# FFN up product of a decoder step as seven half-size block products, with activations and residual through DRAM

## The chip, the cores and the metric

The kernel runs on one core of a Trainium2 chip. The metric is the device time of one execution in microseconds. The core's engines, as the profile names them: PE (TensorE, matmuls; PEld its weight loads), DVE (VectorE), ACT (ScalarE), POOL (GpSimd) and SP (SyncE, which only issues transfers). Each runs its own instructions in order and waits for others through semaphores.

## What is computed

One layer of a decoder for a prompt of 1024 tokens and 8 samples of 8 tokens, 1088 columns in all, with D = 1024 and a hidden width of 4096. The change touches the second half of the layer:

```python
def _layer_tail(x, attn, pool, gate1, shift2, scale2, gate2, norm2_g, w_out, w_up, w_down):
    mix = jnp.concatenate([attn, pool], axis=-1).astype(x.dtype) @ w_out
    x = x + gate1 * mix
    h = rms_norm(x, norm2_g) * (1 + scale2) + shift2
    f = jnp.square(jax.nn.relu(h @ w_up)) @ w_down
    return x + gate2 * f
```

Gates, shifts and scales come from a conditioning vector: one for the prompt, one for each sample.

## The kernel before

Everything is stored with features on the 128 partitions and tokens along the columns. A product in full precision is made of three matmuls on 32-bit operands: each operand is split in a rounded high part and the remainder, and high x high, low x high and high x low are summed in PSUM. `gemm` (L238 to L247) walks over the k tiles of 128 rows and issues the three passes for each column chunk; `CHUNKS` cuts the 1088 columns into 512, 288 and 288, since one PSUM bank holds 512. `load_w` and `split_w` (L143 to L153) fetch a weight tile of 512 KB on SP's queue, copy its high part on ScalarE (L146) and subtract on VectorE (L147); four raw buffers and three pairs of split ones (`NRAW`, `NWF`) rotate.

The tail of the layer begins with the out projection, `out_tile`: eight tiles m on the first 512 columns ("a"), then eight on the other 576 ("b"). `add_gated` (L828 to L836) adds the gated result to the residual `X`, which stays in SBUF to the end, and the squares are summed into `acc2` for the norm. `rstd_of` (L198 to L215) makes 1/rms with one matmul by ones per chunk, Ln and Exp on ScalarE and a Newton step on VectorE. `h2_prompt` (L855 to L859) makes the FFN's input, high and low part, for one k. For the first 512 columns this is done while the "b" tiles run. For the others the norm comes after the last "b" tile, and three up tiles on the first 512 columns (`up_a`) stand in front of it.

Then `up(ff)` makes one of 32 tiles of 128 hidden features: `gemm` over eight k tiles, relu on ScalarE from PSUM (L926), square on VectorE (L927), split (L930, L931) into `fh`, `fl`, which stay in SBUF. Four such tiles make a group; `down(gq)` multiplies the group with its part of `w_down` for each of the eight output tiles m and adds the gated result to `X`. Up tiles and down groups alternate, eight groups in all. `windows(b)` copies two caches of a sample from DRAM to DRAM on POOL's queue, 4080 KB each, one pair per group; a copy of one column to `mark` makes it wait for the group's first tile.

The order of instructions outside the blocks named `manual_schedule` is made by a planner that hoists what is ready; inside such a block the engines named keep the program's order.

## Time and profile before

| | us |
|---|---|
| median of 3 runs | 1374.87 |
| lowest and highest of them | 1372.66, 1382.95 |
| the profiled execution, its own time | 1385.76 |
| span of that execution, first to last instruction | 1384.0 |
| mean granted TensorE clock in it | 0.978 |

The profile is of one execution. Its page gives the busy time of each engine, the chain of waits that ended last, and groups of instructions by line, each with its count, busy time, mean and idle time in front. The timeline lists instructions by start; an entry "x3" is three of a kind merged, and its second figure is the time from the first one's start to the last one's end. A duration holds the engine's latency, so that the next instruction of an engine can begin before it is over: what one costs on a busy engine is the distance between starts.

### The profile page before, as it was taken

What the parts mean: (1) busy time and instruction counts of PE and PEld (TensorE: products, weight loads), DVE (VectorE), ACT (ScalarE), POOL (GpSimd) and SP (SyncE); (2) the same over time, 40 slices, a digit from 0 to 9 for tenths busy, and PEclk for the clock granted to TensorE, in tenths of its full rate; (3) what the DMA queues carried; (4) which work ended last, traced back from release to release, by engine and by line L of the source; (5) the groups of instructions that cost most, each with busy time, mean ns of one, the idle gap of its engine ahead of it and who ended that gap; (6) DMA issues with size and microseconds to landing.
All of it is one profiled execution on the core that took longest, in us unless ns stands there. A gap on an engine that the chain in (4) does not pass through costs nothing.

```text
span 1384.0 us, 21247 instructions
## 1 busy us (share of the span) xinstructions
PE 1325.9 (96%) x9060; PEld 1112.8 (80%) x9060; DVE 584.5 (42%) x1120; ACT 390.1 (28%) x660; POOL 119.0 (9%) x175
## 2 busy tenths in 40 slices
PE   3698999998999999999999999999999999999998
PEld 1485777894665567999999999999999999999998
DVE  5643233314656565577332433432433324334333
ACT  6232030224766653435202202112012012021120
POOL 3201002611212000000000000000000000000000
PEclk9899799998999999999999999999999999999999
DMA  9686433427767563482961541721814615411002
GB/s 322 209 112 170 133 124 125 157 93 287 249 208 268 174 232 113 133 282 70 338 207 46 186 149 47 260 74 45 274 46 133 201 46 186 149 47 46 31 33 97
DMA packets 48719, 211.09 MB, mean 153 GB/s; under 512 B 6432, under 2 KB 6688, under 8 KB 47600
## 3 DMA queue, kind: packets, MB, share of 16 engines
q1 hardware_dynamic: 44752, 137.17, 30.3%
q0 software_dynamic: 3872, 72.56, 16.6%
q8 instruction: 71, 1.16, 0.3%
q14 instruction: 24, 0.20, 0.0%
...
## 4 chain that ended last, share of the span: by engine, by line
PE 90%; DMA 4%; DVE 3%; ACT 2%; issue 1%; SPq 0%; DVEq 0%; ACTq 0%
PE dn L245 9%; PE dn L243 9%; PE dn L247 9%; PE up L245 9%; PE up L247 9%; PE up L243 9%; PE z L243 5%; PE z L247 5%; PE z L245 4%; PE po L715 2%; PE pt L705 2%; PE S L660 2%; PE spo L618 1%; PE pa L101 1%; PE sl L572 1%; PE ob L247 1%
## 5 line engine op out<-in xcount | busy, mean ns | idle before, releaser
L831 DVE SCALAR_TENSOR_TENSOR X<-dn,aT,X 128x512 f32<-128x512 f32 (+2 forms) x192 | 98.4, 568 | 204.5 <-PE dn L247 204.5
L863 POOL COPY mark<-fh 128x1 f32<-128x1 f32 x7 | 8.5, 1218 | 561.9 <-ACT fh L930 561.9
L931 DVE TENSOR_TENSOR fl<-r,fh 128x1088 fp32r<-128x1088 f32 x32 | 41.3, 1292 | 35.5 <-ACT fh L930 35.5
L528 ACT ACTIVATE L<-L,m 128x128 f32<-128x128 f32 (+7 forms) x64 | 49.1, 770 | 19.2 <-DVE m L532 19.2
L708 ACT COPY PT<-pt 128x512 f32<-128x512 f32 (+1 forms) x80 | 41.7, 541 | 39.2 <-PE pt L705 30.4
L705 PE MATMUL pt<-cpk,L 128*128 128x128 f32 x288 | 45.4, 284 | 2.6 <-ACT PT L708 1.5
L930 ACT CAST fh<-r 128x1088 fp32r<-128x1088 f32 x32 | 35.4, 1105 | 44.1 <-DVE r L927 44.1
L705 PEld LDWEIGHTS pt<-cpk,L 128*128 128x128 f32 x288 | 31.2, 141 | 18.0 <-issue 10.9
L245 PE MATMUL dn<-fh,wd_3l 128*128 128x288 f32 (+1 forms) x192 | 43.4, 328 | 0.0
L243 PE MATMUL dn<-fh,wd_3h 128*128 128x288 f32 (+1 forms) x192 | 43.4, 328 | 0.0
L247 PE MATMUL dn<-fl,wd_3h 128*128 128x288 f32 (+1 forms) x192 | 43.4, 328 | 0.0
L243 PE MATMUL dn<-fh,wd_1h 128*128 128x288 f32 (+1 forms) x192 | 42.5, 328 | 0.0
L245 PE MATMUL dn<-fh,wd_1l 128*128 128x288 f32 (+1 forms) x192 | 42.5, 328 | 0.0
L247 PE MATMUL dn<-fl,wd_1h 128*128 128x288 f32 (+1 forms) x192 | 42.3, 328 | 0.0
L245 PE MATMUL dn<-fh,wd_0l 128*128 128x288 f32 (+1 forms) x192 | 42.3, 328 | 0.0
L243 PE MATMUL dn<-fh,wd_0h 128*128 128x288 f32 (+1 forms) x192 | 42.2, 328 | 0.0
L245 PE MATMUL dn<-fh,wd_2l 128*128 128x288 f32 (+1 forms) x192 | 42.2, 328 | 0.0
L243 PE MATMUL dn<-fh,wd_2h 128*128 128x288 f32 (+1 forms) x192 | 42.2, 328 | 0.0
L247 PE MATMUL dn<-fl,wd_2h 128*128 128x288 f32 (+1 forms) x192 | 42.2, 328 | 0.0
L247 PE MATMUL dn<-fl,wd_0h 128*128 128x288 f32 (+1 forms) x192 | 42.1, 328 | 0.0
L927 DVE TENSOR_TENSOR r<-r 128x1088 f32<-128x1088 f32 x32 | 41.1, 1286 | 0.0
L532 DVE CUSTOM_DVE_ANT_0 L<-S,fs 128x384 f32<-128x384 f32 (+5 forms) x64 | 32.0, 538 | 18.7 <-PE S L660 18.5
...
## 6 DMA issues: line engine op xcount, KB each, us to landing
out_kw<-in_cache_k POOLq DMA_DIRECT2D x8, 4080.0 KB, 15.8
out_vw<-in_cache_v POOLq DMA_DIRECT2D x8, 4080.0 KB, 29.2
wa<-in_w_ada SPq DMA_DIRECT2D x48, 512.0 KB, 4.7
kc<-in_kc SPq DMA_DIRECT2D x40, 512.0 KB, 5.1
vc<-in_vc SPq DMA_DIRECT2D x40, 512.0 KB, 4.9
...
fs<-gscr SPq DMA_DIRECT2D x8, 512.0 KB, 7.7
```

Source lines behind the costliest of these rows:

```text
L243: mm(pt[:, :n], wh[:, kw], xh(k, c0, n), start=st, stop=False)
L245: mm(pt[:, :n], wl[:, kw], xh(k, c0, n), start=False, stop=False)
L247: mm(pt[:, :n], wh[:, kw], xl(k, c0, n), start=False, stop=sp)
L528: last["act"] = S.activation(L[:, :n], L[:, :n], AF.Exp, bias=negm, scale=-1.0, accum_out=sm)
L532: V.tensor_tensor_reduce(out=L[:, c0:c0 + n], in0=pt, in1=bias, scale=-1.0, scalar=(3.0e38 if prev is None else prev), op0=ALU.add, op1=AL ...
L660: mm(pts[a][:, :nm], w[r, qc], m[r, c0:c0 + nm], start=(x == 0), stop=(x == 2))
L705: nc.tensor.transpose(pt[:, n * P:(n + 1) * P], u["L"][:, a, ii * nk0 + j * P:ii * nk0 + (j + 1) * P], ident)
L708: later(0, lambda: S.copy(PT[:, :n * P], pt[:, :n * P]))
L831: V.scalar_tensor_tensor(X[:, m, c0:c0 + npr], pt[:, :npr], aT[:, base + m, 0:1], X[:, m, c0:c0 + npr], ALU.mult, ALU.add)
L927: V.tensor_tensor(r, r, r, ALU.mult)
L930: S.copy(fh, r)
L931: V.tensor_sub(fl, r, f(fh))
```

## The change

The up product H = W h is cut in 2 x 2 blocks: W by hidden features (ff and ff + 16) and by k (the first and last four k tiles), h by k and by columns (two halves of 544, `T2`, each in two chunks of 272, `NC`). For each of 16 pairs of hidden tiles the four blocks of the result are made of seven block products (Strassen's scheme in Winograd's form) in place of eight. `prod(m, n)` is one of them, 4 k tiles x 3 passes x 2 chunks = 24 matmuls. Products 1, 6, 7 and 4 of a pair add up in two PSUM banks (X), 5 and 3 in two others (Y), 2 in two more (Z); `hold` copies a sum at a certain point from PSUM to SBUF, `result` adds it to another, squares the relu and writes the tile to DRAM (`uscr`) on POOL's queue. `up_w` makes the weight sums (g = 0: none, 1 and 2: two additions of 512 columns, 3: none, half a tile) and their splits.

The sums of h (T1 to T4) are made once: T1 from both column halves of the first four k tiles, T2 and T4 from those and the last four, T3 from all. They stay in SBUF for all 16 pairs in the space of `X`, so the residual is written to DRAM (`xscr`) by `out_tile` and read back as `X3`. The first two pairs are interleaved product by product, in an order written by hand for PE, DVE and ACT, with the norm of the second half and the making of T1 to T4 between the products (`lagged` issues its steps k by k, each later step `lag` turns behind). From m = 2 on the planner orders the pairs. `down` runs after all of up; its activations are loaded four at a time from `uscr` and split then. The out projection now runs on halves of 544 columns as two chunks of 272. Four cache windows go with pairs 3, 6, 9 and 12, three with down groups 0, 2 and 4.

```diff
+T2 = T // 2
+NC = T2 // 2
+K2 = KD // 2
...
+    XQ = {(a, b): xp.tile([P, K2, T2], F32, tag=f"q{a}{b}", name=f"X{a}{b}") for b in range(2) for a in range(2)}
+    def X(k, c0, n):
+        h = c0 // T2
+        return XQ[k // K2, h][:, k % K2, c0 - h * T2:c0 - h * T2 + n]
+    for b in range(2):
+        for k in range(KD):
+            nc.sync.dma_start(X(k, b * T2, T2), i["xT"][k][:, b * T2:(b + 1) * T2])
+    rstd2 = xp.tile([P, T], F32, tag="rstd2", name="rstd2")
...
+    xscr = tc.dram_tile([KD, P, T], F32, name="xscr")
+    uscr = tc.dram_tile([NFF, P, T], F32, name="uscr")
+    bp = tc.alloc_tile_pool(name="bp", bufs=1, side="right", reuse_waits="tile")
+    B1 = [[bp.tile([P, K2, T2], F32R, tag=f"B{k}{n}", name=f"B{k}{n}") for n in "hl"] for k in range(2)]
...
+        G.dma_start(xscr[m][:, a0:a1], X(m, a0, a1 - a0))
+    def split(hi, lo, src):
+        S.copy(hi, src)
+        V.tensor_sub(lo, src, f(hi))
+    def h2_rows(k, half):
+        c0 = half * T2
+        n = min(T2, SEQ - c0)
+        x = X(k, c0, n)
+        V.scalar_tensor_tensor(x, x, A2[:, k, 0:1], rstd2[:, c0:c0 + n], ALU.mult, ALU.mult)
+        S.activation(x, x, AF.Identity, bias=aT[:, 24 + k, 0:1])
...
+    HALF = [((c, NC), (c + NC, NC)) for c in (0, T2)]
     for m in range(KD):
-        out_tile(m, CHUNKS[:1], "a")
-    out_tile(0, CHUNKS[1:], "b")
-    rstd_of(acc2, rstd2, CHUNKS[:1], "n2a")
+        out_tile(m, HALF[0], "a")
+    out_tile(0, HALF[1], "b")
+    rstd_of(acc2, rstd2, HALF[0], "n2a")
     for m in range(1, KD):
-        out_tile(m, CHUNKS[1:], "b")
+        out_tile(m, HALF[1], "b")
         if m == 1:
             windows(0, rstd2[:, 0:1])
             for k in range(KD):
...
-    rstd_of(acc2, rstd2, CHUNKS[1:], "n2b")
...
+                h2_rows(k, 0)
+                split(B1[k // K2][0][:, k % K2], B1[k // K2][1][:, k % K2], X(k, 0, T2))
...
+    raws, wts = {}, {}
+    def up_raw(m):
+        raws[m] = []
+        for x in range(2):
+            raw = wpool.tile([P, 1024], F32, tag="raw", name=f"wu{m}_{x}r", bufs=NRAW)
+            nc.sync.dma_start(raw, i["w_up"][m + x * NFF // 2])
+            raws[m].append(raw)
+    def up_w(m, g):
+        top, bot = raws[m]
+        a11, a12, a21, a22 = top[:, :512], top[:, 512:], bot[:, :512], bot[:, 512:]
+        if g == 0:
+            src, n = top, 1024
+        elif g == 3:
+            src, n = a22, 512
+        elif g == 1:
+            src, n = wpool.tile([P, T], F32, tag="tmp", name=f"ws{m}", bufs=2)[:, :1024], 1024
+            V.tensor_add(src[:, :512], a21, a22)
+            V.tensor_sub(src[:, 512:], src[:, :512], a11)
+            s2[m] = src[:, 512:]
+        else:
+            src, n = top, 1024
+            V.tensor_sub(a11, a11, a21)
+            V.tensor_sub(a12, a12, s2[m])
+        hi = wpool.tile([P, 1024], F32R, tag="wf", name=f"wu{m}_{g}h", bufs=NWF)
+        lo = wpool.tile([P, 1024], F32R, tag="wf", name=f"wu{m}_{g}l", bufs=NWF)
+        S.copy(hi[:, :n], src)
+        V.tensor_sub(lo[:, :n], src, f(hi[:, :n]))
+        wts[m, g] = hi, lo
+    s2, ops = {}, {1: (0, 0), 2: (0, 512), 5: (1, 0), 6: (1, 512), 7: (2, 0), 3: (2, 512), 4: (3, 0)}
+    bs2 = {1: B1[0], 2: B1[1]}
+    banks, held = {}, {}
+    def bank(m, x):
+        if (m, x) not in banks:
+            banks[m, x] = [ps(f"u{x}{m}_{c}", "px" if x == "X" else "pyz") for c in range(2)]
+        return banks[m, x]
+    def hold(m, n, src):
+        held[m, n] = []
+        for c in range(2):
+            t = fr.tile([P, NC], F32, tag=f"held{n}{c}", name=f"h{n}_{m}_{c}", bufs=1 if n == 1 else 2)
+            S.copy(t, src[c][:, :NC])
+            held[m, n].append(t)
+    def result(m, x, half, src, with_):
+        r = fr.tile([P, T2], F32, tag="rt", name=f"r{m}_{x}{half}", bufs=NRT)
+        for c in range(2):
+            dst = r[:, c * NC:(c + 1) * NC]
+            if with_ is None:
+                S.copy(dst, src[c][:, :NC])
+            else:
+                V.tensor_add(dst, src[c][:, :NC], held[m, with_][c])
+        V.scalar_tensor_tensor(r, r, 0.0, r, ALU.max, ALU.mult)
+        G.dma_start(uscr[m + x * NFF // 2][:, half * T2:(half + 1) * T2], r)
+    START = {1: "X", 5: "Y", 2: "Z"}
+    HOME = {1: "X", 6: "X", 7: "X", 4: "X", 5: "Y", 3: "Y", 2: "Z"}
+    def prod(m, n):
+        x = HOME[n]
+        g, w0 = ops[n]
+        hi, lo = wts[m, g]
+        bh, bl = bs2[n]
+        outs = bank(m, x)
+        for k in range(K2):
+            kw = slice(w0 + k * P, w0 + (k + 1) * P)
+            for w, b in ((hi, bh), (lo, bh), (hi, bl)):
+                for c in range(2):
+                    mm(outs[c][:, :NC], w[:, kw], b[:, k, c * NC:(c + 1) * NC], start=(START.get(n) == x and k == 0 and w is hi and b is bh),
+                       stop=(k == K2 - 1 and b is bl), skip_group_check=(n in (6, 7, 3, 4)))
+        if n == 1:
+            hold(m, 1, outs)
+        elif n == 5:
+            hold(m, 5, outs)
+        elif n == 6:
+            hold(m, 6, outs)
+        elif n == 2:
+            result(m, 0, 0, outs, 1)
+        elif n == 7:
+            result(m, 1, 1, outs, 5)
+        elif n == 3:
+            result(m, 0, 1, outs, 6)
+        else:
+            result(m, 1, 0, outs, None)
...
+    for m in range(2):
+        up_raw(m)
+        up_w(m, 0)
+    up_w(0, 1)
...
+    bs2.update({5: (T1h, T1l), 6: (T2h, T2l), 7: (T3h, T3l)})
...
+    with tc.manual_schedule(engines={mybir.EngineType.PE, mybir.EngineType.DVE, mybir.EngineType.Activation}):
+        prod(0, 1)
+        vt = wpool.tile([P, T], F32, tag="tmp", name="n2bv", bufs=2)
+        vv, tv = vt[:, :T2], vt[:, T2:]
+        for c0, n in HALF[1]:
+            pp = ps(f"n2b_{c0}", "pyz")
+            mm(pp[:, :n], ones, acc2[:, c0:c0 + n], start=True, stop=True)
+            V.tensor_scalar(vv[:, c0 - T2:c0 - T2 + n], pp[:, :n], 1.0 / D, EPS, ALU.mult, ALU.add)
+        S.activation(tv, vv, AF.Ln)
+        S.activation(rstd2[:, T2:], tv, AF.Exp, scale=-0.5)
+        newton(rstd2[:, T2:], vv, tv)
+        prod(0, 2)
+        rsb = rstd2[:, SEQ:T].rearrange("p (b t) -> p b t", t=TS).unsqueeze(1).to_broadcast([P, K2, NB, TS])
+        def samples(a):
+            V.tensor_tensor(xsq[a], xsq[a], rsb, ALU.mult)
+            V.tensor_tensor(xsq[a], xsq[a], bs_seq(A2, K2 * a), ALU.mult)
+            V.tensor_tensor(xsq[a], xsq[a], bs_seq(aT, 24 + K2 * a), ALU.add)
+        samples(0)
+        lagged((0, lambda j: h2_rows(j, 1)),
+               (1, lambda j: V.tensor_sub(B(j, 0), B(j, 1), B(j, 0))),
+               (1, hi_of(T1h, lambda j: B(j, 0))),
+               (2, lo_of(T1h, T1l, lambda j: B(j, 0))))
+        prod(1, 1)
+        up_w(0, 2)
+        prod(1, 2)
+        up_w(1, 1)
+        prod(0, 5)
+        samples(1)
+        lagged((0, lambda j: h2_rows(K2 + j, 1)),
+               (1, lambda j: V.tensor_sub(B(j, 0), B(K2 + j, 1), B(j, 0))),
+               (1, hi_of(T2h, lambda j: B(j, 0))),
+               (2, lambda j: V.tensor_sub(B(K2 + j, 0), B(K2 + j, 0), B(j, 0))),
+               (2, lo_of(T2h, T2l, lambda j: B(j, 0))))
+        prod(1, 5)
+        prod(0, 6)
+        lagged((0, lambda j: V.tensor_sub(B(j, 1), B(K2 + j, 1), B(j, 1))),
+               (0, hi_of(T3h, lambda j: B(j, 1))),
+               (1, lo_of(T3h, T3l, lambda j: B(j, 1))))
+        prod(1, 6)
+        prod(0, 7)
+        up_w(1, 2)
+        B4h, B4l = [xp.tile([P, K2, T2], F32R, tag=t, name=n) for t, n in (("q00", "B4h"), ("q01", "B4l"))]
+        bs2[3] = B4h, B4l
+        lagged((0, hi_of(B4h, lambda j: B(K2 + j, 1))), (0, lo_of(B4h, B4l, lambda j: B(K2 + j, 1))))
+        prod(1, 7)
+        prod(0, 3)
+        up_w(0, 3)
+        T4h = xp.tile([P, K2, T2], F32R, tag="q11", name="T4h")
+        bs2[4] = T4h, T4l
+        lagged((0, hi_of(T4h, lambda j: B(K2 + j, 0))), (0, lo_of(T4h, T4l, lambda j: B(K2 + j, 0))))
+        prod(1, 3)
+        prod(0, 4)
+        up_w(1, 3)
+    up_raw(2)
+    up_w(2, 0)
+    prod(1, 4)
+    up_w(2, 1)
...
+    NM = NFF // 2
+    for m in range(2, NM):
+        last = m == NM - 1
+        if not last:
+            up_raw(m + 1)
+        for n in (1, 5, 6, 2, 7, 3, 4) if not last else (1, 2, 5, 6, 7, 3, 4):
+            prod(m, n)
+            if n == 1 and m in (3, 6, 9, 12):
+                windows(m // 3, held[m, 1][0][:, 0:1])
+            if n == 5:
+                up_w(m, 2)
+            elif n == 2 and not last or last and n == 6:
+                up_w(m, 3)
+            elif n == 7 and not last:
+                up_w(m + 1, 0)
+            elif n == 3 and not last:
+                up_w(m + 1, 1)
...
+    def load_f(ff, pool):
+        raw = fb.tile([P, T], F32, tag="fraw", name=f"f{ff}r", bufs=FG)
+        nc.sync.dma_start(raw, uscr[ff])
+        fh = pool.tile([P, T], F32R, tag="fh", name=f"fh{ff}", bufs=FG)
+        fl = pool.tile([P, T], F32R, tag="fl", name=f"fl{ff}", bufs=FG)
+        split(fh, fl, raw)
+        fs_[ff] = (fh, fl)
...
+    for ff in range(FG):
+        load_f(ff, fa)
+    X3 = fb.tile([P, KD, T], F32, tag="X3", name="X3")
     for k in range(KD):
...
-        fh = fr.tile([P, T], F32R, tag="fh", name=f"fh{ff}", bufs=NFR)
-        fl = fr.tile([P, T], F32R, tag="fl", name=f"fl{ff}", bufs=NFR)
...
+        nc.sync.dma_start(X3[:, k, :], xscr[k])
...
+            if mp == 0 and gq + 1 < NFF // FG:
+                for ff in range((gq + 1) * FG, (gq + 2) * FG):
+                    load_f(ff, fa if gq % 2 else fb)
...
     for gq in range(NFF // FG):
-        while nxt < min(NFF, (gq + 1) * FG + 1):
-            up(nxt)
-            nxt += 1
...
-            windows(gq + 1, f(fs_[gq * FG][0][:, 0:1]))
         down(gq)
-    fr.release()
+        if gq in (0, 2, 4):
+            windows(5 + gq // 2, f(fs_[(gq + 2) * FG - 1][0][:, 0:1]))
...
-NFR = 5
+NRT = 4
```

## Rows read from the trace of the kernel before

**Rows 1.** The page: busy time of each engine, and the chain that ended last, by engine.

```profile
PE 1325.9 (96%) x9060; PEld 1112.8 (80%) x9060; DVE 584.5 (42%) x1120; ACT 390.1 (28%) x660; POOL 119.0 (9%) x175
...
PE 90%; DMA 4%; DVE 3%; ACT 2%; issue 1%; SPq 0%; DVEq 0%; ACTq 0%
```

**Rows 2.** The windows view: a stretch in us, its length, then busy us and count of PE, PEld, DVE, ACT, POOL, the granted clock, the DMA engines' busy share and GB/s. The first stretch is a part of the "b" tiles, the second the whole FFN.

```profile
590.00:600.00 10.00, 10.00 (x77) 10.00 (x76) 10.00 (x18) 4.68 (x7) 0.00 (x0) 1.00 0.98 325
...
618.30:1384.00 765.70, 761.84 (x4614) 692.97 (x4612) 290.52 (x477) 146.56 (x204) 15.03 (x21) 1.00 0.38 123
```

**Rows 3.** The timeline: start us, length us, engine, line, what. First the "a" tiles' ends by VectorE's addition, then TensorE in a "b" tile, the next one, the first up tile, and two down tiles that lie two apart.

```profile
533.83 0.75 DVE L831 SCALAR_TENSOR_TENSOR X<-oa,aT,X 128x512 f32<-128x512 f32 x1 [3.36 <-PE oa L247]
...
539.27 0.75 DVE L831 SCALAR_TENSOR_TENSOR X<-oa,aT,X 128x512 f32<-128x512 f32 x1 [2.75 <-PE oa L247]
...
605.49 0.43 PE L243 MATMUL ob<-mixh,wob6h 128*128 128x288 f32 x2
...
611.89 0.43 PE L243 MATMUL ob<-mixh,wob7h 128*128 128x288 f32 x2
...
618.29 0.39 PE L243 MATMUL up<-h2ah,wu0h 128*128 128x512 f32 x1
...
785.84 0.67 PE L243 MATMUL dn<-fh,wd_1h 128*128 128x512 f32 x3
...
797.76 0.67 PE L243 MATMUL dn<-fh,wd_2h 128*128 128x512 f32 x3
```

**Rows 4.** The timeline around the second half's norm, on VectorE (the last out tile's reads of PSUM, and the Newton steps), TensorE and ScalarE.

```profile
618.51 0.87 DVE L831 SCALAR_TENSOR_TENSOR X<-ob,aT,X 128x288 f32<-128x288 f32 x2
619.30 0.22 DVE L834 TENSOR_TENSOR gs<-ob,aT 128x64 f32<-128x64 f32 x1
...
623.89 1.13 PE L205 MATMUL n2b<-acc,cpk 128*128 128x288 f32 x4
624.64 0.61 PE L243 MATMUL up<-h2ah,wu1h 128*128 128x512 f32 x1
...
625.59 1.28 ACT L209 ACT_TABLE_LOAD   x1 [4.03 <-DVE n2bv L206]
...
627.59 1.28 ACT L212 ACT_TABLE_LOAD   x1
...
631.19 0.76 DVE L135 SCALAR_TENSOR_TENSOR rstd<-n2bt,rstd 128x576 f32<-128x576 f32 x1
```

**Rows 5.** Groups by line and form, VectorE then ScalarE: busy us, mean ns of one | idle before.

```profile
L931 DVE TENSOR_TENSOR fl<-r,fh 128x1088 fp32r<-128x1088 f32 x5 | 6.4, 1291 | 3.5 <-ACT fh L930 3.5
...
L926 ACT ACTIVATE r<-up 128x288 f32<-128x288 f32 x10 | 3.5, 408 | 0.0
...
L146 ACT CAST wu0h<-wu0r 128x1024 fp32r<-128x1024 f32 x1 | 1.0, 1049 | 4.9 <-DMA wu0r<-in_w_up 4.9
...
L908 ACT CAST h2bh<-hs 128x512 fp32r<-128x512 f32 x1 | 0.6, 623 | 0.5 <-DVE hs L906 0.5
```

**Rows 6.** The timeline of VectorE: starts of a subtraction of 512 columns and its next, of a PSUM read of 288 and its next, of a weight subtraction of 1024 and its next, and of a 512-column tensor-tensor and its next.

```profile
592.89 0.74 DVE L859 SCALAR_TENSOR_TENSOR h2al<-h2p,aT,h2ah 128x512 fp32r<-128x512 f32 x1
593.55 0.51 DVE L831 SCALAR_TENSOR_TENSOR X<-ob,aT,X 128x288 f32<-128x288 f32 x1
593.98 0.74 DVE L857 SCALAR_TENSOR_TENSOR h2p<-X,A,rstd 128x512 f32<-128x512 f32 x1
...
601.37 1.23 DVE L147 TENSOR_TENSOR wob7l<-wob7r,wob7h 128x1024 fp32r<-128x1024 f32 x1
602.51 0.22 DVE L836 TENSOR_TENSOR X<-X,gs 128x64 f32<-128x64 f32 x1
...
631.98 0.69 DVE L903 TENSOR_TENSOR hs<-X,rstd 128x512 f32<-128x512 f32 x1
632.59 0.74 DVE L857 SCALAR_TENSOR_TENSOR h2p<-X,A,rstd 128x512 f32<-128x512 f32 x1
```

**Rows 7.** The windows view (columns as in rows 2) of a stretch early in the kernel, where TensorE has nothing to do for 3.8 us.

```profile
129.00:132.80 3.80, 0.00 (x0) 0.00 (x0) 3.73 (x4) 0.00 (x0) 0.00 (x0) 0.90 1.00 378
132.80:136.00 3.20, 3.11 (x18) 0.83 (x18) 2.51 (x7) 2.13 (x4) 0.00 (x0) 0.50 0.07 27
...
148.00:152.00 4.00, 4.00 (x14) 3.58 (x14) 0.00 (x0) 0.00 (x0) 0.53 (x1) 0.50 0.93 332
152.00:156.00 4.00, 4.00 (x24) 3.63 (x23) 1.23 (x1) 1.05 (x1) 0.00 (x0) 0.93 0.32 129
```

**Rows 8.** DMA issues: out<-in, issuing queue, count, KB each, median us from issue to landing.

```profile
out_kw<-in_cache_k POOLq DMA_DIRECT2D x8, 4080.0 KB, 15.8
out_vw<-in_cache_v POOLq DMA_DIRECT2D x8, 4080.0 KB, 29.2
...
wd_1r<-in_w_down SPq DMA_DIRECT2D x8, 512.0 KB, 3.7
...
wu1r<-in_w_up SPq DMA_DIRECT2D x1, 512.0 KB, 22.7
```

**Rows 9.** The timeline of SP's queue at the out projection's start: a weight load (which comes after X in the program) and X's eight.

```profile
503.37 0.33 SPq L152 DMA_DIRECT2D woa4r<-in_w_out  x1
...
509.37 4.09 SPq L820 DMA_DIRECT2D X<-in_xT  x8
```

More of the change, by code (lines that the diff above doesn't have):

```diff
@@ L835, in add_gated, with out_tile @@
                             aT[:, base + m, 1:9].unsqueeze(2).to_broadcast([P, NB, TS]), ALU.mult)
-            V.tensor_add(X[:, m, SEQ:T], X[:, m, SEQ:T], t.rearrange("p b t -> p (b t)"))
+            x = X(m, SEQ, NS)
+            V.tensor_add(x, x, t.rearrange("p b t -> p (b t)"))
     acc2 = nat("acc2")
-    rstd2 = xp.tile([P, T], F32, tag="rstd2", name="rstd2")
-    def out_tile(m, chunks, name, split=None):
+    def out_tile(m, chunks, name):
         a0, a1 = chunks[0][0], chunks[-1][0] + chunks[-1][1]
@@ L893, in body @@
-    rstd_of(acc2, rstd2, CHUNKS[1:], "n2b")
-    up_a(1)
-    up_a(2)
+                h2_rows(k, 0)
+                split(B1[k // K2][0][:, k % K2], B1[k // K2][1][:, k % K2], X(k, 0, T2))
+    pools[""].release()
+    pools[""] = tc.alloc_tile_pool(name="psum4", bufs=1, space=PSUM, reuse_waits="tile")
+    raws, wts = {}, {}
[5 more added lines that the diff above has]
+            raws[m].append(raw)
@@ new lines, in body, with lagged @@
+    bs2.update({5: (T1h, T1l), 6: (T2h, T2l), 7: (T3h, T3l)})
+    xsq = [XQ[a, 1][:, :, SEQ - T2:].rearrange("p k (b t) -> p k b t", t=TS) for a in range(2)]
+    hi_of = lambda hi, src: lambda j: S.copy(hi[:, j], src(j))
+    lo_of = lambda hi, lo, src: lambda j: V.tensor_sub(lo[:, j], src(j), f(hi[:, j]))
+    B = lambda k, half: X(k, half * T2, T2)
+    def lagged(*stages):
+        for t in range(K2 + max(lag for lag, _ in stages)):
+            for lag, st in stages:
+                if 0 <= t - lag < K2:
+                    st(t - lag)
@@ new lines, in body @@
+    bp.release()
+    fa = tc.alloc_tile_pool(name="fa", bufs=1, side="right", reuse_waits="tile")
+    fs_ = {}
+    def load_f(ff, pool):
[5 more added lines that the diff above has]
+        fs_[ff] = (fh, fl)
+    fr.release()
+    pools[""].release()
@@ L934, in down @@
+    pools[""] = tc.alloc_tile_pool(name="psum5", bufs=8, space=PSUM, reuse_waits="tile")
+    fb = tc.alloc_tile_pool(name="fb", bufs=1, side="left", reuse_waits="tile")
+    for ff in range(FG):
+        load_f(ff, fa)
+    X3 = fb.tile([P, KD, T], F32, tag="X3", name="X3")
+    for k in range(KD):
+        nc.sync.dma_start(X3[:, k, :], xscr[k])
     def down(gq):
```

79 lines of the change are left out of this document (15 added, 64 removed).

## Prediction

> **What bounds the kernel now.** I read the page's busy lines and the windows first: over the span TensorE is busy 1325.9 of 1384.0 us [rows 1], and from the first up product (618.3) to the end 761.84 of 765.70, at a granted clock of 1.00; VectorE is busy only 290.5 us there and ScalarE 146.6 [rows 2]. The chain of waits agrees: 90% of what ended last is TensorE [rows 1]. So the FFN stage is bound by the number and spacing of its matmuls, and there is no idle time to win back; a change gains only by fewer or narrower matmuls, and loses by every gap that it opens.
>
> Next the timeline, for the spacing. A 512-column matmul of the out projection costs 5.44/24 = 226.7 ns (tile to tile, 533.83 to 539.27), a 288-column one 6.40/48 = 133.3 ns (605.49 to 611.89), and the mixed group 512+288+288 of the down product 11.92/24 = 496.7 ns (785.84 to 797.76) [rows 3]. The straight line through the first two is N/2.4 + 13.3 ns. Up and down are 64 tiles of 24 groups: 64 x 11.92 = 762.9 us. 618.3 + 762.9 leaves 2.8 us of 1384.0: 0.75 for the norm's matmuls at 623.89 [rows 4] and a tail of some 2.
>
> **The change part by part**, against this execution (span 1384.0 us).
>
> *Fewer products.* 16 column pairs x 7 products x 4 k x 3 passes x 2 chunks = 2688 matmuls of 272 columns, for 2304 that were wider. By the line one takes 272/2.4 + 13.3 = 126.7 ns. A product is 24 of them, 3.04 us; a round of seven 21.3; all 112 take 340.5 us for 381.4: -40.9. The bounds: the plain column share of the 288 row, 125.9 ns (-43), and no gain at all from the narrower form, 133.3 ns (-23.1). I take the line, since 272 lies beside 288. The Trainium skill (TensorE: Matmul & The Clock Gate, Back-to-back issue gap) gives a warm gap of N/2.4 + 2.5 ns; by it a product would be an estimated 2.78 us and 112 of them 311 us. The trace differs: at 512 columns it has 226.7 ns where that rule gives 215.8, so the measured line stands.
>
> *Out projection* in four 272s for 512+288+288: 24 x 506.8 ns = 12.16 us a tile for 5.44 + 6.40: +0.32 x 8 = +2.6.
>
> *The start of the FFN* is where I expect the gain to go. Products 1 and 2 of a pair need only the first half of the columns. Product 5 needs T1, 6 needs T2, 7 needs T3, and these need the second half's norm and a run of VectorE and ScalarE work, in an order written by hand, so that every engine goes in program order. Before, the second half's operands took two VectorE operations per k, and three up tiles on the first 512 columns covered them.
>
> Prices, from durations [rows 5] and start to start where the next doesn't wait [rows 6]: tensor-tensor 0.61 at 512 columns and 1.14 at 1024, so 0.65 at 544; scalar-tensor-tensor 0.66 at 512, so 0.62 at 480 and 0.70 at 544; a PSUM read of 272 0.43; one that waits for the one before it costs its whole duration. ScalarE: 1.05 for a 1024 copy, 0.62 for 512, 0.41 for 288 from PSUM. So a result (two PSUM adds, then the squared relu) is 1.6; a weight sum (two 512 adds, copy, 1024 subtraction, each behind the last) 3.6; the sample columns 1.3; T1 three VectorE operations for each of 4 k, 8.2 with its first and last waits; T2 with T4 four each, 10.7; T3 two each, behind ScalarE's copies, 5.9.
>
> From the end of the out projection (0): product 1 writes the banks of the last out tile, whose PSUM reads end 1.2 us later [rows 4]. It ends at 4.3. The norm's chain (matmul, two table loads of 1.28, Ln, Exp, three Newton steps) took 623.89 to 631.95 = 8.1 us [rows 4]: 12.3. Then VectorE in order: result (0,2) 13.9, samples 15.2, T1 23.4, weight sum 27.0, result (1,2) 28.6, weight sum (1,1) 32.3, samples 33.6, T2/T4 44.3, T3 50.2. TensorE has its four ready products done at 14.0, idles to 18.0, ends (0,5) with T1 at 23.7, waits to 31.2 for the weights of (1,5), ends (0,6) with T2 at 44.6, (1,6) 47.6, (0,7) 50.6; then (1,7) waits for result (0,7) and its weight sum, 55.9, and ends at 58.6; three products at their rate, 67.8; the last one's 512-column split, behind a result, at 70.1; end at 72.9. The same 14 products and the norm are 43.3 us of work: +29.6. The bounds: VectorE's bare work alone, nothing waiting (six results 9.6, samples 2.6, T1 to T4 23.1, the splits of B4 and T4 5.2, weights 8.2, norm and a last relu 3.8), is some 53 us behind the 5 us at the front: 58, +15; and waits longer than I count, +35.
>
> To this comes the clock. After 3.8 us without a matmul (129.0 to 132.8) the grant fell to 0.50, the 1.2 GHz level, though TensorE was busy again from 132.8 on, and stayed there through 15 us of sparse matmuls and the dense ones of 148 to 152; from 152 to 156 it was 0.93 [rows 7]. The gaps at 14.0, 23.7 and 50.6 are 4, 7.5 and 4.2 us. The first two are covered by VectorE's work, which then sets the pace. [...]
>
> *Weight sums later.* A round has 12 us of VectorE work (5632 columns of weight sums and splits at 1.1 ns, 6.2; results 5.5) and 7 of ScalarE (3584 columns of weight copies, 3.7; eight copies from PSUM, 3.3) in 21.3; holds and results have one product, 3 us, between them and the next writer of their bank. I take nothing for that; if VectorE is in the midst of a 1.14 us subtraction, the 3 us still cover it.
>
> *Scratch writes and windows.* Result writes go on POOL's queue, as do the eight cache windows (two copies of 4 MB). kw lands after 15.8 us and vw after 29.2, so they go one behind the other; a weight load issued beside the first window took 22.7 us, later ones 3.7 [rows 8]. In rounds 3, 6, 9 and 12 the window is issued some 5 us in and lands at 35; the results of that round land behind it at 36 to 39, and the next round needs the first of the four result buffers at 33.5. VectorE waits 2.5 us, the sums behind it are late, product 4 by about 1: 4 x 1 = +4 (0 to 24). Weight loads of the round after next land with the window, at 35, and are wanted at 36: no slack, no cost. The Trainium skill (DMA: Bandwidth & Descriptors, Queues, rings and completion order) says that each DMA engine takes the descriptors of one ring in order; this would put the result writes behind the window, and kw and vw agree with that. If they could slip past, this term were 0 and the sum 4 us less.
>
> *Up to down.* X3 is read back from scratch and the first eight activations go through a scratch load of 2.2 MB and a split (1.1 + 1.3 us each [rows 5]), from buffers free after the last round's third product, 12 us ahead. That SP's queue isn't held by X3, which waits for T3, I take from the out projection: a weight load that follows X in the program was issued ahead of X's eight [rows 9]. The last result's PSUM copies hold the third bank for 1.5 us; in the last round 7 comes right behind 6 and waits 1 for its copies: +2.5 (up to +12 if the first scratch load waits for the last scratch write). Later loads hide under a down group, 8 x 5.96 = 47.7 us.
>
> Sum: -40.9 + 2.6 + 29.6 + 3.5 + 4.0 + 2.5 = +1.3. The profiled span lies 9.1 us above the median of the runs shown (1374.87, 1372.66 to 1382.95); carried over, 1374.87 + 1.3 = 1376.2. About 1% is what a measurement of this kernel can tell from no change, 13.7 us.
>
> **The rivals.**
> - *The start is cheaper, faster.* ScalarE's copies and the waits run beside other VectorE work, the clock doesn't fall, and the start costs the bare 58 us: -14.9 - 3.5 = 1357.8. For it: between 590 and 600 VectorE was busy 10.00 of 10 us in work of this kind [rows 2]. Against it: a hand-written order puts each subtraction right behind the copy that it waits for.
> - *Windows stall the rounds, slower.* If the result writes or weight loads land over 3 us later than counted, product 4 or the next round's product 1 waits for the rest: at 6 us a window 24 for 4, 1396.2. It decides where a result write lands over 39 us into its round. For it: the weight load of 22.7 us; against: those loads stopped no matmul before, and a buffer is still one product ahead.
> - *Narrow matmuls cost as much as 288s*, so the eighth isn't had: +17.7 and +2.6, 1396.5. For it: only a fixed cost bigger than 13.3 ns; the two widths measured speak against it.
> - *Scratch read waits for the last write*: +9.5, 1385.7, still within 1%.
>
> **How the numbers follow.** Forecast 0.42, cheap start 0.24, windows 0.19, narrow matmuls 0.07, scratch wait 0.08. The likeliest one's own range is 1365 to 1388, by the clock's and the start's smaller errors. Faster 0.25 (the cheap start and the forecast's lower edge), same 0.48 (forecast and scratch wait), slower 0.27 (windows, narrow matmuls, a little of the forecast). The range goes from 1355 (the cheap start with some of its spread) to 1396 (windows), and leaves out 2 in 10: the far ends of both.
>
> **What would show it.** Right: some 72 to 77 us from the end of the out projection to the first product of round 2, with TensorE idle before (0,5), (1,5) and (1,7) and released by VectorE; dense rounds of 21.3 us; a granted clock under 1.00 only in that start. Wrong: products of 3.0 us without a gap from the first on (cheap start), 3.2 us each (narrow matmuls), rounds 4, 7, 10 and 13 longer by 4 us and more (windows), or a gap before the first down tile.

## The result, and the profile after

The changed kernel takes 1390.15 us (1380.38 to 1395.51), the kernel before 1374.85 beside it: ratio 1.0085, 95% interval 1.0062 to 1.0109, some 11.7 us slower. Its profiled run has a span of 1388.5 us. Stages are compared from the first output tile on (863.0 us before, 874.2 after), since the parts ahead of it, which the change leaves alone, differ by several us between any two profiled runs.

The page of the changed kernel, busy time and the chain by engine, as in [rows 1]: TensorE is busy 27 us less in a longer span, and VectorE's part of the chain has gone from 3% to 7%.

```profile
PE 1298.7 (94%) x9638; PEld 1125.2 (81%) x9638; DVE 710.6 (51%) x1383; ACT 435.1 (31%) x751; POOL 158.6 (11%) x255
...
PE 83%; DVE 7%; DMA 6%; ACT 3%; issue 1%; SPq 0%; DVEq 0%; ACTq 0%
```

The windows view of the changed kernel by stage (columns as in [rows 2]): out projection, start (rounds 0 and 1), the other rounds, then the wait and the down product; below it 90 us of the rounds.

```profile
514.34:612.16 97.82, 97.82 (x772) 97.44 (x772) 55.94 (x98) 39.30 (x53) 9.20 (x18) 1.00 0.59 200
612.16:692.60 80.44, 54.92 (x341) 51.56 (x342) 62.02 (x100) 34.34 (x57) 4.54 (x9) 0.85 0.19 67
692.60:988.67 296.07, 295.65 (x2354) 295.22 (x2352) 160.45 (x250) 88.29 (x170) 34.94 (x67) 1.00 0.62 217
988.67:1388.50 399.83, 385.70 (x2304) 350.90 (x2304) 193.09 (x384) 66.10 (x63) 4.98 (x12) 0.98 0.48 168
...
693.00:783.00 90.00, 90.00 (x720) 90.00 (x719) 49.53 (x77) 26.96 (x53) 11.38 (x22) 1.00 0.55 191
```

The rounds are dense: 720 matmuls in 90.00 us are 125.0 ns each, a product 3.0 us, a round 21.0. The start is not: its 14 products and the norm's 0.75 us are 42.75 us of work in 80.44, at a mean granted clock of 0.85. Of the 37.7 us on top TensorE waits 25.5 (80.44 less 54.92 busy); in the other 12.2 it is busy longer than that work takes in the rounds. Most of this lies in four products. The windows view of (0,1), (0,5) and (1,5), with 24 matmuls each:

```profile
616.89:622.47 5.58, 5.58 (x24) 5.58 (x25) 2.49 (x6) 1.71 (x2) 0.54 (x1) 0.50 0.15 53
637.08:643.50 6.42, 6.25 (x24) 5.55 (x24) 6.26 (x10) 3.75 (x8) 0.00 (x0) 0.51 0.00 0
649.73:655.04 5.31, 4.87 (x24) 4.46 (x24) 5.11 (x9) 2.55 (x6) 0.00 (x0) 0.64 0.00 0
```

With (1,7), whose 5.6 us are shown further on, TensorE is busy 21.5 us in four products that take 12.0 at a clock of 1.00. Each follows a wait of 3.8 to 6.1 us.

What TensorE waited for in the changed kernel: us in total, times, longest.

```profile
PE dn L246 <- ACT fh L868: 10.3, 1, 10.3
PE uY L977 <- ACT wu_1h L930: 6.1, 1, 6.1
PE uX L977 <- DVE X L842: 4.7, 1, 4.7
...
PE uY L977 <- ACT T1h L1004: 4.3, 1, 4.3
PE uX L977 <- ACT wu_2h L930: 3.8, 1, 3.8
PE uX L977 <- DVE T2l L1005: 3.7, 4, 1.5
...
PE uX L977 <- ACT wu_3h L930: 1.2, 1, 1.2
```

Read with the timeline, these are places: the first down product (10.3), (1,5) behind its weight sum (6.1), the first product behind the last residual add (4.7), (0,5) behind T1 (4.3), (1,7) (3.8) and (1,4) (1.2) behind weight sums, and T2's four steps.

The ledger against the kernel before: products 2688 x 125.0 ns = 336.0 for 381.4, -45.4; out projection 97.82 for 97.31, +0.5; start 80.44 - 42.75 = +37.7; rounds 296.07 for 14 x 21.0, +2.1; the wait ahead of the down product +10.3; the down product itself 389.6 for 32 x 11.92 and a tail of 2, +6.1. Sum +11.3, as the spans have it. Of the 6.1, 1.9 is no loss: from the last matmul to the end it is 3.9 us in both kernels, not 2. Some 3.2 is the clock, which was 0.53 in the first 6.6 us behind the wait:

```profile
998.93:1005.54 6.61, 6.61 (x22) 5.89 (x23) 5.15 (x4) 3.30 (x3) 0.00 (x0) 0.53 1.02 415
```

The wait of 10.3 us is read on SP's queue, changed kernel:

```profile
981.07 0.33 SPq L155 DMA_DIRECT2D wd_0r<-in_w_down  x1
...
990.91 0.33 SPq L155 DMA_DIRECT2D wd_2r<-in_w_down  x1
991.40 0.39 SPq L1099 DMA_DIRECT2D f0r<-uscr  x1
...
993.66 7.77 SPq L1113 DMA_DIRECT2D X<-xscr  x7
```

The first activation load is issued at 991.40, right behind three weight loads of the second down group, each of which waited for the split that frees its buffer. It lands 6.4 us later, and its split follows.

### The profile page after: what moved, and what is told of

The parts are those of the page before. It is cut to its first block, busy times and chain, and to the rows that moved or that the text cites. A ratio compares the mean times of both kernels' runs of the same rounds, so it can differ in the third digit from the quotient of the medians.

```text
span 1388.5 us, 23225 instructions
## 1 busy us (share of the span) xinstructions
PE 1298.7 (94%) x9638; PEld 1125.2 (81%) x9638; DVE 710.6 (51%) x1383; ACT 435.1 (31%) x751; POOL 158.6 (11%) x255
## 4 chain that ended last, share of the span: by engine, by line
PE 83%; DVE 7%; DMA 6%; ACT 3%; issue 1%; SPq 0%; DVEq 0%; ACTq 0%
PE uX L977 14%; PE dn L246 9%; PE dn L248 9%; PE dn L250 9%; PE uY L977 7%; PE z L246 5%; PE z L250 5%; PE z L248 4%; PE uZ L977 3%; PE pt L708 2%; PE po L718 2%; PE S L663 2%; PE pa L104 1%; PE spo L621 1%; PE sl L575 1%; DMA wu_0r<-in_w_up 1%
## 5 line engine op out<-in xcount | busy, mean ns | idle before, releaser
L961 POOL DMA_DIRECT2D uscr<-r x64 | 34.8, 544 | 320.5 <-DVE r L960 318.1
L246 PE MATMUL dn<-fh,wd_0h 128*128 128x288 f32 (+1 forms) x192 | 43.3, 334 | 10.3 <-ACT fh L868 10.3
L960 DVE SCALAR_TENSOR_TENSOR r<-r 128x544 f32<-128x544 f32 x64 | 45.8, 721 | 4.9 <-ACT r L957 4.0
L931 DVE TENSOR_TENSOR wu_3l<-wu_1r,wu_3h 128x512 fp32r<-128x512 f32 x16 | 11.1, 691 | 70.2 <-ACT wu_3h L930 70.2
L708 PEld LDWEIGHTS pt<-cpk,L 128*128 128x128 f32 x288 | 31.3, 142 | 18.0 <-issue 10.9
L246 PEld LDWEIGHTS dn<-fh,wd_0h 128*128 128x128 f32 x192 | 33.3, 192 | 13.4 <-ACT fh L868 10.5
```

The lines of the kernel that those rows point to most:

```text
L246: mm(pt[:, :n], wh[:, kw], xh(k, c0, n), start=st, stop=False)
L708: nc.tensor.transpose(pt[:, n * P:(n + 1) * P], u["L"][:, a, ii * nk0 + j * P:ii * nk0 + (j + 1) * P], ident)
L960: V.scalar_tensor_tensor(r, r, 0.0, r, ALU.max, ALU.mult)
L961: G.dma_start(uscr[m + x * NFF // 2][:, half * T2:(half + 1) * T2], r)
```

## The experiments

Stage times below go from the last output tile to the first product of round 2 ("start", 80.4 us in the changed kernel), or on to the last up product ("up", 376.5).

**Operand sums left out.** Products 5, 7 and 4 take B1's first half, 6 and 3 its second; the norm, the rows and T1 to T4 are gone.

```diff
-    bs2.update({5: (T1h, T1l), 6: (T2h, T2l), 7: (T3h, T3l)})
+    bs2.update({5: B1[0], 6: B1[1], 7: B1[0], 3: B1[1], 4: B1[0]})
```

> Leaves work out: the second half's norm, its rows and T1 to T4 with B4 are not made; products (m,5), (m,7) and (m,4) multiply the first-half rows 0 to 3 instead, (m,6) and (m,3) rows 4 to 7. All matmuls, weight sums, results and transfers stay. Theory (the start's stall of 37.9 us is the hand-ordered VectorE and ScalarE chain behind the operand sums): the 14 products of rounds 0 and 1 run in 42 us plus the first wait of 4.7 us plus up to 4 us of waits for weight sums, so the stage goes from 80.6 to 47 to 51 us and the time falls by 30 to 34 us, to 1356 to 1360. Rival (the start is held by the weights' loads and their splits as well, so it only trades one wait for another): the stage stays above 60 us and the time falls by less than 20 us.

Measured 1368.5 us, ratio 0.9959 (0.9935 to 0.9983); windows view, start:

```profile
610.06:671.50 61.44, 49.48 (x338) 48.18 (x338) 28.45 (x45) 13.33 (x24) 4.33 (x8) 0.89 0.25 88
```

19.0 us by the stages (by the ratios some 17), not 30 to 34: the theory as stated falls, and what its rival said came true, a stage above 60 us and a time less than 20 us shorter. The operand sums are half of the stall. TensorE still waits 4.2 us for the last residual add and 3.9 for the weight sum of (1,7), with VectorE now busy only 28.45 us. These two are other stalls, and the next two runs take one each; beside them TensorE is busy 49.5 us in 14 products that take 42.0 at a clock of 1.00, as the mean clock is 0.89.

**First window later.**

```diff
-            windows(0, rstd2[:, 0:1])
...
-            if n == 1 and m in (3, 6, 9, 12):
-                windows(m // 3, held[m, 1][0][:, 0:1])
+            if n == 1 and m in (2, 5, 7, 9, 12):
+                windows((2, 5, 7, 9, 12).index(m), held[m, 1][0][:, 0:1])
```

> The same work; the first of the cache windows is started in round 2 instead of in the second output tile, the later ones in rounds 5, 7, 9 and 12. Theory (the first product waited 4.7 us instead of 1.2 since the last weight loads of the start landed behind the window's 45 us of transfers, which delayed a split that stood ahead of the last residual add on VectorE): the wait falls to 1 to 2 us, time lower by 2.5 to 4 us, 1386 to 1388. Rival (the loads are late for buffers or the scratch writes): no change, within 1 us of 1390.

1383.84 us, ratio 1.0067 (1.0043 to 1.0092). In the changed kernel ScalarE waited 1.75 us for a weight load of the start, and the split behind it stood ahead of the residual add on VectorE:

```profile
614.03 1.04 ACT L930 CAST wu_0h<-wu_0r 128x1024 fp32r<-128x1024 f32 x1 [1.75 <-DMA wu_0r<-in_w_up]
...
615.11 1.23 DVE L931 TENSOR_TENSOR wu_0l<-wu_0r,wu_0h 128x1024 fp32r<-128x1024 f32 x1 [2.07 <-ACT wu_0h L930]
616.25 0.84 DVE L842 SCALAR_TENSOR_TENSOR X<-ob,aT,X 128x272 f32<-128x272 f32 x2
```

With the window later, TensorE's wait for that add, and the windows view of the start:

```profile
PE uX L976 <- DVE X L842: 0.6, 1, 0.6
```

```profile
607.34:680.98 73.64, 52.33 (x341) 49.02 (x341) 60.05 (x98) 33.06 (x55) 4.32 (x8) 0.88 0.18 58
```

The start is 6.8 us shorter, twice the forecast: besides the wait of 4.7, now 0.6, product (0,1) takes 3.1 us instead of 5.6, as TensorE has not stood idle ahead of it. The theory holds, but its price was short of the clock, and the window's transfers take some 29 us from issue, not 45. The gain is read from the stages of one profiled execution; the two ratios, 1.0067 and 1.0085, are only 2.5 us apart, inside their intervals.

**Weight sums ahead of results.**

```diff
         prod(0, 6)
+        up_w(1, 2)
         lagged((0, lambda j: V.tensor_sub(B(j, 1), B(K2 + j, 1), B(j, 1))),
...
         prod(0, 7)
-        up_w(1, 2)
...
+        up_w(1, 3)
         prod(1, 3)
         prod(0, 4)
-        up_w(1, 3)
```

> The same work; two of the hand-ordered weight sums of the start stand earlier on VectorE: that of (1,7) and (1,3) ahead of T3 instead of behind the result of (0,7), that of (1,4) ahead of product (1,3) instead of behind the result of (0,4). Theory (part of the stall is not the operand sums' length but a weight sum queued behind a result that waits for TensorE, with the lower granted clock behind that idle stretch): the wait of 3.8 us ahead of (1,7) goes, (1,7) and (0,7) together take 6 to 8 us instead of 12.7, the wait of 1.2 us ahead of (1,4) goes; the stage from the last output tile to round 2 goes from 80.6 to 73 to 76 us, time lower by 5 to 7 us, 1383 to 1385. Rival (VectorE is full up to there, so the sums only push T3 and the wait moves to (0,7)): the stage stays within 2 us of 80.6.

1382.93 us, ratio 1.0053 (1.0027 to 1.0079). VectorE in the changed kernel, around this place:

```profile
666.84 1.58 DVE L1005 TENSOR_TENSOR T3l<-X,T3h 128x544 fp32r<-128x544 f32 x2
669.06 0.79 DVE L959 TENSOR_TENSOR r<-uX,h 128x272 f32<-128x272 f32 x2 [0.64 <-PE uX L977]
...
670.53 0.68 DVE L926 TENSOR_TENSOR wu_0r<-wu_0r,wu_1r 128x512 f32<-128x512 f32 x1
...
672.92 1.23 DVE L931 TENSOR_TENSOR wu_2l<-wu_0r,wu_2h 128x1024 fp32r<-128x1024 f32 x1 [1.11 <-ACT wu_2h L930]
```

The sum begins only at 670.53, behind a result that waits for (0,7). With the sums ahead that wait is gone, 1.4 us at T3 take its place, and the start is 75.6 us, -4.8, as foreseen.

**Filler matmuls.**

```diff
+            mm(banks[m, "Y"][x % 2][:, NC:512], wts[1, 1][0][:, :P], B1[0][0][:, 0, :512 - NC], start=False, stop=False, skip_group_check=True)
...
+        filler(1, 30)
         prod(1, 7)
```

> Adds work: 30 matmuls of 240 columns into unread columns of an idle bank, some 3.4 us, in the idle stretch of 3.8 us ahead of product (1,7). Theory (the granted clock of 0.59 to 0.84 right behind that stretch makes (1,7) 5.6 us long instead of 3.0, and nothing hides that, as all products behind it are ready): (1,7) ends 1.5 to 2.5 us earlier, time lower by that, 1387.5 to 1388.5. Rival (product (1,7) is long since its weights' low part comes late, not for the clock): no change or up to 1 us more.

1390.85 us, ratio 1.0124 (1.0100 to 1.0148). Windows view; first the changed kernel in the idle stretch and in (1,7), then the kernel with the filler in the same two places, and ahead of them.

```profile
669.00:673.00 4.00, 0.20 (x3) 0.06 (x1) 2.79 (x6) 1.15 (x2) 0.54 (x1) 1.00 0.19 70
673.00:679.00 6.00, 5.25 (x28) 5.04 (x29) 4.92 (x7) 4.88 (x9) 0.00 (x0) 0.72 0.26 87
```

```profile
656.70:669.60 12.90, 9.47 (x49) 8.75 (x49) 12.01 (x19) 6.74 (x13) 0.00 (x0) 0.74 0.00 1
...
672.70:676.60 3.90, 3.49 (x31) 3.30 (x30) 2.73 (x6) 1.09 (x2) 0.54 (x1) 1.00 0.19 71
676.60:681.00 4.40, 3.64 (x27) 3.43 (x28) 3.76 (x5) 3.28 (x7) 0.00 (x0) 1.00 0.36 123
```

With the stretch filled, the clock behind it stays at 1.00 (2.4 GHz) instead of 0.72, and (1,7) takes 4.1 us instead of 5.6. That much is as foreseen. But in this run the clock is 0.74 in (0,6) and (1,6), where the changed kernel had 1.00, and the start is 82.7 us. The theory holds for (1,7), but nothing is gained in the total, where it foresaw 1387.5 to 1388.5: filling one gap did not mend a start that has several.

**Two low parts on POOL.**

```diff
-        V.tensor_sub(lo[:, :n], src, f(hi[:, :n]))
+        lo_eng.tensor_sub(lo[:, :n], src, f(hi[:, :n]))
...
-        up_w(0, 2)
+        up_w(0, 2, G)
...
-        up_w(1, 1)
+        up_w(1, 1, G)
```

> The same work; the low parts of two weight sums of the start, those of (0,7)/(0,3) and (1,5)/(1,6), are made by POOL instead of VectorE (1.22 us each there). Theory (from the first result to T3 VectorE works without gaps and its sum sets when T2 and T3 are ready): T2 and T3 are ready 2.4 us earlier and (1,7) starts 2 to 2.5 us earlier; the stage from the last output tile to round 2 goes from 80.6 to 78 us. Rival (the chain runs through ScalarE's copies or the matmuls at the lower granted clock): within 0.7 us of 80.6; or, if POOL's slower subtraction (2.8 us) ends last at (1,5), up to 1.6 us longer.

1390.2 us, ratio 1.0098 (1.006 to 1.0135); "up" 376.2 us. No gain. The timeline, POOL and VectorE, shows why:

```profile
644.15 2.44 POOL L931 TENSOR_TENSOR wu_2l<-wu_0r,wu_2h 128x1024 fp32r<-128x1024 f32 x1 [10.82 <-ACT wu_2h L930]
...
644.31 2.83 DVE L921 TENSOR_TENSOR ws<-wu_1r 128x512 f32<-128x512 f32 x1
647.17 0.69 DVE L922 TENSOR_TENSOR ws<-ws,wu_0r 128x512 f32<-128x512 f32 x1
```

A VectorE addition of 0.69 us that starts beside POOL's subtraction lasts until it ends, 2.83. The second pair does the same, so VectorE saves 2.4 us and loses 4.2. The Trainium skill (SBUF — State Buffer, Who interferes with whom) says that a VectorE instruction with two SBUF inputs and a GpSimd one that reads SBUF exclude each other; the trace agrees.

**Scratch loads first.**

```diff
+            with tc.issue_after(after.ins):
+                nc.sync.dma_start(raw, src)
...
-            wh, wl = load_w(i["w_down"][gq, mp], f"wd{gq}_{mp}")
+            wh, wl = load_w(i["w_down"][gq, mp], f"wd{gq}_{mp}", after=x3 if gq == 1 else None)
```

> The same work; on SP's queue the weight loads of the second down group stand behind the first four loads of the activations and the eight of the residual, instead of ahead of them. Theory (the 10.3 us between the last up product and the first down product is SP's order: the activation loads stood behind weight loads that waited for buffers): the four loads issue at 976 to 983 us of the span instead of 991.4, the gap falls from 10.3 to under 3 us, and the two slow down tiles behind it get back up to 3 us: time lower by 7 to 12 us, 1378 to 1383. Rival (the loads wait for the scratch writes of the last round, or for the buffers of the products): they issue where they did, the gap stays at 8 to 10 us, time within 2 us of 1390.

1379.59 us, ratio 1.0042 (1.0016 to 1.0069). SP's queue:

```profile
970.06 0.33 SPq L1103 DMA_DIRECT2D f0r<-uscr  x1
...
979.29 3.82 SPq L1117 DMA_DIRECT2D X<-xscr  x8
...
987.39 0.47 SPq L157 DMA_DIRECT2D wd_0r<-in_w_down  x1
```

The first load goes out 12.9 us ahead of the last up product (982.94). The wait falls from 10.3 to 2.3 us, which is about the 2.5 that the prediction had for this place, and the stretch behind it from 389.6 to 386.8: 10.8 us by the stages, as foreseen; the two ratios are 5.9 us apart, each with an interval of some 3.5 us either way.

**The three mends together** (the edits above).

> The scratch loads first, the windows later and the sums ahead in one kernel. Theory (three separate stalls, so their stage times add: 10.9 us by the profile of the scratch loads first, 6.8 of the windows later, 5 to 7 of the sums ahead): 22 to 25 us less than the changed kernel, 1365 to 1368, ratio to the kernel before 0.992 to 0.995. Rival (they overlap, the chain on VectorE takes up what one of them frees): 12 to 17 us less, 1373 to 1378, no faster than before.

1366.98 us, ratio 0.9928 (0.9897 to 0.9959), faster than before. The start is 69.1 us, 11.3 less, for 6.8 + 4.8: the stalls add.

**A plain start.** Rounds 0 and 1 as eight plain products each; T1 to T4 are made behind them. The core of the edit:

```diff
+        whole(1, 0, 0)
+        whole(1, 1, 0)
+        lagged((0, lambda j: h2_rows(K2 + j, 1)), (1, hi_of(T2h, b4)), (2, lo_of(T2h, T2l, b4)))
...
+        lagged((0, sub_on(G, b2, b4, b2)))
+        lagged((0, sub_on(G, b3, b3, b1)))
...
+        whole(1, 1, 1)
```

> The output is the same; rounds 0 and 1 are not made of seven products but of eight plain ones each (16 instead of 14), so that their first 24 us need only first-half rows and no sums, and T1 to T4 are made behind them for round 2; six of the sums' stages are on POOL; windows later and scratch loads first as in those two runs. Theory (the start's stall is that the seven products need all operand sums within two rounds; spread over four rounds they hide): the stage from the last output tile to round 2 is 49 us of products and 1 to 5 us of waits instead of 80.6, round 2 is at most 4 us longer than 21, the gap ahead of the down products 2 to 3 us: 36 to 42 us less than the changed kernel, 1348 to 1354, ratio 0.981 to 0.986. Rival (VectorE and ScalarE cannot make it in that time either, so the stall moves into rounds 2 and 3): round 2 and 3 take over 10 us more than 42 and the time stays above 1362.

1364.42 us, ratio 0.9911 (0.9877 to 0.9946). The 16 products run in 50.0 us at a clock of 1.00, so the start's stall is gone, as the theory says:

```profile
609.45:659.60 50.15, 49.24 (x391) 48.98 (x389) 41.39 (x51) 22.84 (x40) 19.82 (x15) 1.00 0.16 50
```

The total misses the 1348 to 1354 foreseen by some 10 us, and its ratio is not clear of the 0.9928 of the three mends. Round 2 waited 3.6 us for a hold behind a weight sum, and the down product 4.4 us for an activation behind a window. The eight subtractions on POOL took up to 1.8 us each and stretched VectorE's beside them (timeline; the last row starts just before POOL's next):

```profile
642.54 3.45 POOL L1053 TENSOR_TENSOR X<-X,X 128x544 f32<-128x544 f32 x2
...
644.70 1.89 DVE L1053 TENSOR_TENSOR X<-X,X 128x544 f32<-128x544 f32 x1
646.51 0.71 DVE L1018 TENSOR_TENSOR T1l<-X,T1h 128x544 fp32r<-128x544 f32 x1
```

**All sums on VectorE**, with the sixth window in round 13; and, as a contrast, the same with T3's and T4's sums on POOL.

```diff
-        lagged((0, sub_on(G, b2, b4, b2)))
+        lagged((0, sub_on(V, b2, b4, b2)))
...
+        sums(3)
         prod(2, 3)
```

> As the plain start, with all operand sums on VectorE instead of POOL, the weight sums of rounds 2 and 3 ahead of results that wait for TensorE, and the sixth window started in round 13 instead of beside the down product. Theory (the plain start fell short for VectorE slowed to 1.88 us for each subtraction of 0.72 while POOL subtracted, a hold queued on ScalarE behind a weight sum, 3.6 us, and one activation load behind a window, 4.4 us): its waits of 3.6, 1.6 and 4.4 us go, the stretch from the last output tile to the last up product goes from 357.7 to 349 to 352 us and the down stretch is 4 us shorter: 8 to 13 us less than the plain start, 1352 to 1357, ratio 0.981 to 0.985. Rival (VectorE is too full without POOL): new waits of the same size in rounds 2 and 3, time within 4 us of 1364.

> As the plain start with all sums on VectorE, but the eight subtractions that make T3 and T4 are on POOL. Theory (POOL and VectorE hold each other up where both have two operands in memory): VectorE's operations beside them take 1.5 to 2.9 us instead of 0.7, so VectorE loses as much as POOL takes from it (8 x 0.64 = 5.1 us), and TensorE waits are up by 0 to 4 us; time 0 to 4 us above the kernel with all on VectorE. Rival (work taken off VectorE shortens its chain): VectorE's operations stay at 0.7 us and the time is 0 to 4 us lower.

1382.31 us, ratio 1.0051 (1.0028 to 1.0073), and 1380.41, 1.0016 (0.9988 to 1.0045). Both theories on the first missed. Rounds 0 to 2 are as foreseen, but "up" is 377.7 us, and the waits lie where neither looked, in rounds 4 and 10. Of the first kernel, the waits of TensorE and of VectorE, and the result writes during the window issued at 827 us (count, KB each, median us to landing):

```profile
PE uY L989 <- DVE r L971: 10.9, 1, 10.9
...
DVE r L971 <- DMA uscr<-r: 29.8, 7, 11.2
```

```profile
uscr<-r POOLq DMA_DIRECT2D x4, 272.0 KB, 28.7
```

VectorE waits for a result buffer that a late write holds: the windows rival of the prediction, in another kernel. The four writes go out within 3.7 us, from 828.57 to 832.22, right behind the window, and the next result wants a buffer at 846, 17 us after the first of them; it gets one at 857.1. VectorE's load by the sums does not explain it: the contrast, with T3's and T4's sums on POOL, waits as long, while the plain start before, which has these on POOL too, waits 0.6 us at most. The waits of the contrast:

```profile
PE uY L989 <- DVE r L971: 10.7, 1, 10.7
...
DVE r L971 <- DMA uscr<-r: 27.4, 7, 11.0
```

So what the two share is an order of the rounds that bunches results behind a window; which of the edits that both have brought it about was not tried. On POOL, the contrast stretched eight VectorE operations by 1.2 us each to take 8 x 0.64 off, as its theory says; its time came out 2 to 5 us lower, on the side of its rival, but the times of the pair differ by less than the intervals.

**Two cures for that**, each on the kernel with all sums on VectorE: windows issued from ScalarE's queue; six result buffers.

```diff
-        ins = G.tensor_copy(mark, src)
+        ins = S.copy(mark, src)
...
-            G.dma_start(o["vw"][b], i["cache_v"][b, TS * H * E:])
+            S.dma_start(o["vw"][b], i["cache_v"][b, TS * H * E:])
```

```diff
-NRT = 4
+NRT = 6
```

> As the plain start with all sums on VectorE, with the windows issued from ScalarE's queue instead of POOL's, so that the result writes no longer share a queue with them. Theory (what cost that kernel its gain is the result writes standing behind a window's 8 MB in POOL's queue: four result buffers stay taken for up to 28 us and VectorE waits for one, 4.6 us in round 4 and 10.9 us in round 10): a result write lands in under 8 us during a window, those waits go, the stretch from the last output tile to the last up product falls from 377.7 to 353 to 359 us and the time from 1382 to 1358 to 1365 us, ratio 0.986 to 0.992. Rival (it is the DMA engines' share, not the queue): writes still land after 13 us or more, the waits stay, time within 5 us of 1382.

> As the plain start with all sums on VectorE, with six result buffers instead of four; the windows stay on POOL's queue. Theory (the result buffers are what VectorE waits for behind a window): the writes land as late as before, 13 us or more during a window, but the waits of 4.6 and 10.9 us go, the same 353 to 359 us and 1358 to 1365 us. Rival (the hold-up is another one that shows up as a wait for a result): the waits stay and the time is within 5 us of 1382.

1353.46 us, ratio 0.9845 (0.9804 to 0.9885), and 1351.98, 0.9824 (0.9792 to 0.9855): the fastest two, 21 and 24 us under the kernel before. "Up" is 352.4 and 355.0 us, and TensorE has no wait for a result over 0.6 us left. VectorE's wait for the writes with ScalarE's queue, that kernel's writes in the window issued at 731 us, and VectorE's wait with six buffers:

```profile
DVE r L971 <- DMA uscr<-r: 8.7, 3, 3.1
```

```profile
uscr<-r POOLq DMA_DIRECT2D x4, 272.0 KB, 18.6
```

```profile
DVE r L971 <- DMA uscr<-r: 7.3, 1, 7.3
```

Six buffers settle it: behind the last five windows the writes still land 21 to 22 us after issue (29.9 behind the first), and the stall goes. The own queue ends the stall as well, but not for the reason given: its writes land after 17.6 to 20.5 us (21.4 at the first window), not under 8. The 28.7 above is of writes bunched right behind their window, so it is no fair measure beside the 18.6; against six buffers on the shared queue the own one saves 1 to 3 us a window, and 8 at the first. With no window a write lands after some 3 us, so most of the delay is there from either queue: the transfers' share of the DMA engines, as it seems, more than the queue's order. The Trainium skill (DMA: Bandwidth & Descriptors, Queues, rings and completion order) says that an engine takes a ring in order and goes round between the queues packet by packet; that agrees with a gain that is not whole.

## Why the prediction was right or wrong

The time lies in the range and within 1% of before, and in outline the mechanism was the one forecast: the start and the seam to the down product eat what the eighth product saves. The centre, 1376.2, is 14 us low by the medians, just past the forecast's own 1365 to 1388, and 10 by the ledger (+11.3 for +1.3). That is a balance of larger errors: products, out projection and rounds came 8.5 us cheaper than counted, start and seam 18.5 dearer. That these cancelled in part is luck. One of the prediction's own signs of being wrong, a gap before the first down tile, was there. Its terms:

- *Products* -40.9: measured -45.4. The line through two widths gave 126.7 ns for 272 columns; they take 125.0, under the lower bound of 125.9 too, so a round is 21.0 us and not 21.3. The rival of narrow matmuls falls.
- *Out projection* +2.6: +0.5, by the same rate and since the stage before had a clock of 0.98.
- *Start and clock* 29.6 + 3.5: measured 37.7, a start of 80.4 us where 72 to 77 were to show it right. The waits named, ahead of (0,5), (1,5) and (1,7), are there, though they end with ScalarE's copies, which stand behind VectorE's work, and not with VectorE itself; the cheap start isn't. No run shows the 3.5 us that the sum has for the clock: what was slow is the four products above, busy 9.5 us longer than at 1.00 ((1,6) was not among them), of which some may have run beside a chain on VectorE that would have set the pace anyway. What was missed is the first product: it came 4.7 us after the last tile, not 1.2, since weight loads behind the first window held up a split that VectorE's order put ahead of the residual add. With the clock behind it that is 6.8 us by the stages. Another 4.8 was no length of work but a weight sum queued behind a result. The prediction had counted that place (50.6 to 54.8) as given; it could be moved.
- *Windows* +4: no cost. Result writes land 22 us after issue in a window, as counted, but VectorE waited only once, 0.7 us: a round's four results are written within 14 us, and the next comes 17 to 18 us after the last of them. This slack is thin: with another order of results in the rounds it was used up, 10.9 us at one place.
- *Up to down* +2.5: 10.3, and 6.1 in the down product behind it, of which some 3.2 is the clock at 0.53 (so the start was not the only place under 1.00, as had been forecast) and 1.9 the tail, there before as well. This is the step that failed. From [rows 9] I took it that SP's queue would not be held by X3, and so that it would not be held at all. X3 did not hold it; the second down group's weight loads did, put ahead of the activations as the weight load of [rows 9] was put ahead of X. The rival that the read waits for the last scratch write gives the size, but not the cause: moved ahead, the loads went out 12.9 us before the end of the last up product, and 2.3 us of wait are left, the 2.5 counted.

What stays open: the share of the clock in the 37.7 us. The fall behind an idle stretch and its cure are shown at two products (5.6 to 3.1 and to 4.1 us), but runs differ in where else it falls, and no run held the clock up through a whole start of seven products. How much of the cure of the late writes is the queue, and how much the changed moments of writing, is not separated either. Nor was it tried whether the plain start with both cures gains more, or whether six buffers would add to the three mends.
